# Pair sums of w_up made during attention and kept in HBM, and five pairs by seven products in four up chunks

## The chip, the cores and the metric

The kernel runs on one core of one Trainium2 chip. A time is the device time of one execution in microseconds (us). The five engines of the core (TensorE or PE, VectorE or DVE, ScalarE or ACT, GpSimd or POOL, SyncE or SP) each take their own list of instructions in order; semaphores join them. TensorE writes to PSUM, 8 banks of 512 float32 in each of 128 partitions; the other data lie in SBUF.

## The reference

One decoder layer over 256 tokens of width 2048, all in float32:

```python
h = _rmsnorm(x, norm_attn_pre)
proj = h @ w_in                      # 2048 x 4160: A.q, A.k, A.v, c_q, c_kv, k_rope
...                                  # A: dilated window attention, B: latent attention, 8 heads each
x = x + _rmsnorm(mixed @ w_out, norm_attn_post)
h = _rmsnorm(x, norm_mlp_pre)
u = jnp.square(jax.nn.relu(h @ w_up))          # w_up 2048 x 8192
x = x + _rmsnorm(u @ w_down, norm_mlp_post)    # w_down 8192 x 2048
```

## The kernel before, in words

**Products in three passes.** Each float32 matrix is split into a rounded part `hi` and a rest `lo`: ScalarE makes `hi` (L293, with a gain L297), VectorE makes `lo` (L294, with a gain L298). A product is three matmuls, hi by hi, hi by lo and lo by hi (`three`, L983).

**The weight stream.** `Weights` (L154) holds a list of all weight tiles of the program in order of use, each 128 x 1024. `emit` (L178) loads a tile on SP's queue into one of five `raw` buffers and writes its split into one of eight pairs of `hi` and `lo`; `get` (L209) does that for the tile in use and the six after it. So the loads and splits of a tile stand in the lists of their engines where TensorE is six tiles earlier.

**Stages.** First come the projection of x, the heads of A beside the later projections, the latent projections with the heads of B beside them, and the product with w_out. Then follow the up stage and the down stage. The up stage computes h @ w_up in eight chunks of 1024 columns (`j`), each over 16 tiles of 128 rows (`k`); the results of a chunk lie in four banks (two token blocks, two halves of 512 columns).

**Seven products.** In chunks 1 to 7 rows 2k and 2k+1 of w_up for k = 0, 1, 2 are taken as a pair: a 2 x 2 product of blocks (two row tiles by two token blocks by two halves) is made of seven block products instead of eight (`seven_products`, L988), each by three passes. That needs sums of blocks on both sides. The left sums, of h, are made once, in chunk 0, by `left_sums` (L958); they also put the gain into h for the rows they cover (L965). The right sums, of the weights, are made for each pair in each chunk by `seven` (L333): two row tiles are loaded on POOL's queue into the tile `ab` (L360), VectorE makes `t` (L345) and then `u` (L349, L350), and four tiles of the weight stream are made from them: half of the first row tile, the second row tile, u and t. Four extra banks `m` collect those products that several blocks share, and `close` (L1002) adds them up behind the last pair of a chunk; `up_evac` (L905) then adds the result to the accumulators, takes relu, has TensorE transpose it and squares it. `UP_STEPS` (L97) is the order in chunks 1 to 7: plain tiles 6 to 10, pair 0, 11, 12, pair 1, 13, pair 2, 14, 15. A plain tile is 12 matmuls, a pair 21.

**What sets the order.** The schedule is written by hand. `Flow` (L115) runs chains of small steps (Python generators) beside the main line of matmuls; a step yields the number of us, in a rough clock that adds a constant for each matmul, after which its next step is put into the program. All engine lists follow from that clock, which only places instructions and does not time them on the chip. `prelude` (L531) loads x into the tiles `xs`; `powers` (L811) scales them by powers of two before `residual` (L832) adds the attention's result.

Of the kernel before, what the change touches and what calls it, by code (L numbers as in the profile page):

```python
# [18 lines left out]
F32 = mybir.dt.float32  # L19
F32R = mybir.dt.float32r  # L20
# [74 lines left out]

N_SEVEN, SUMS_AHEAD = 3, 2
UP_STEPS = [("k", k) for k in range(6, 11)]  # L97
for _i, _n in enumerate(((11, 12), (13,), (14, 15))):
    UP_STEPS += [("w", _i)] + [("k", k) for k in _n]

# [150 lines left out]
def layer(nc, tc, io):  # L251
# [78 lines left out]

    late = {}

    def seven(load, targets):  # L333

        st, tt, H = {}, nc.vector.tensor_tensor, 512

        def sums():
            ab = load()  # L340
            a, b = st["a"], st["b"] = [ab[:, :CW], ab[:, CW:]] if not isinstance(ab, list) else ab
            t, u = st["t"], st["u"] = targets()
            if not isinstance(ab, list):
                two = [x.rearrange("p (k n) -> p k n", n=H) for x in (t, ab)]
                tt(out=two[0], in0=two[1][:, 0:2, :], in1=two[1][:, 1:4:2, :], op=OP.add)  # L345
            else:
                for x, o in ((a, 0), (b, H)):
                    tt(out=t[:, o:o + H], in0=a[:, o:o + H], in1=x[:, H:], op=OP.add)
            tt(out=u[:, :H], in0=t[:, :H], in1=b[:, H:], op=OP.add)  # L349
            tt(out=u[:, H:], in0=u[:, :H], in1=b[:, :H], op=OP.add)  # L350
# [12 lines left out]
    def seven_up(j, kp):  # L363
        def load():
            if j == FF // CW - 1 and kp:
                return [weights.load(up_weight(j, 2 * kp + i), CW, f"raw_w{j}_{kp}{i}") for i in range(2)]
            return load_two(late["ab"], nc.gpsimd if (j, kp) > (1, 0) else nc.sync,
                            io["w_up"][2 * kp * P:(2 * kp + 2) * P, j * CW:(j + 1) * CW])

        return seven(load, lambda: [late["up"].tile([P, CW], F32, tag="T", bufs=2, name=f"{n}{j}_{kp}") for n in "tu"])  # L370
# [30 lines left out]
    wide_u, after = [], 0  # L401
    for j in range(FF // CW):
        wide_u.append([])
        for what, k in [("k", k) for k in range(KD)] if j == 0 else UP_STEPS:
            if what == "k":
                ts = [weights.plan(up_weight(j, k), 1, CW, gcol[:, 8 + k:9 + k])]
# [124 lines left out]
    def prelude():  # L531
# [15 lines left out]
        rstd0.append(rstd_of(ss0, NB, D, "pre"))  # L547

    def tables():

# [98 lines left out]

    pre = flow.start(prelude())  # L650
    tab = flow.start(tables())
    heads, evacs = [], []
    for half in range(2):
# [157 lines left out]
    def powers():  # L811
# [93 lines left out]
    def up_evac(j, b, i, acc, order, more=None):  # L905
# [11 lines left out]
        if j not in uT:  # L917
            if j in (12, 13):
                t2 = late["ab"][:, (j - 12) * CW:(j - 11) * CW]
            else:  # L920
# [37 lines left out]
    def left_sums(kp):  # L958
# [7 lines left out]
        four_sums(q, f)  # L966
        st = [late["st"][:, i * 512:(i + 1) * 512] for i in (2 * kp, 2 * kp + 1)]
        yield 3.0
# [19 lines left out]
    def seven_products(ts, left, accs, m, first, last):  # L988
# [4 lines left out]
        for p, (a, i, half, to) in enumerate(prods):  # L993
            w = weights.get(ts[i])
# [21 lines left out]
    for j in range(FF // CW):  # L1016
# [9 lines left out]
        for t, b in order:  # L1026
            what, k, tiles = steps[t]
            if (j, t, b) == (0, 8, 0):
# [11 lines left out]
            if j == 1 and what == "w":  # L1040
                flow.until(lambda: len(sums) > k)
# [12 lines left out]

            first, last = k == 0, k == N_SEVEN - 1
            if first:
# [205 lines left out]
```

## Time and profile before

| | us |
|---|---|
| median of 3 runs | 1055.2 (1055.2 to 1055.52) |
| span of the profiled execution | 1053.8 |
| TensorE busy | 1040.8 |
| VectorE busy | 811.1 |
| ScalarE busy | 625.1 |
| GpSimd busy | 61.5 |

The span runs from the first to the last instruction that was profiled. Matmuls overlap in the pipeline, so a single one reads some 0.39 us where the next starts after 0.23. In the lists of groups a line ends with busy time, mean ns of one, and the idle time of the engine ahead of it with what ended it. In a table of windows the columns are the window, its length, then for each engine the busy time with the number of instructions, the granted clock of TensorE, the share of the DMA engines that was busy, and GB/s.

### The profile page before, as it was taken

What the parts mean: (1) busy time and instruction counts of PE and PEld (TensorE: products, weight loads), DVE (VectorE), ACT (ScalarE), POOL (GpSimd) and SP (SyncE); (2) the same over time, 40 slices, a digit from 0 to 9 for tenths busy, and PEclk for the clock granted to TensorE, in tenths of its full rate; (3) what the DMA queues carried; (4) which work ended last, traced back from release to release, by engine and by line L of the source; (5) the groups of instructions that cost most, each with busy time, mean ns of one, the idle gap of its engine ahead of it and who ended that gap; (6) DMA issues with size and microseconds to landing.
All of it is one profiled execution on the core that took longest, in us unless ns stands there. A gap on an engine that the chain in (4) does not pass through costs nothing.

```text
span 1053.8 us, 13458 instructions
## 1 busy us (share of the span) xinstructions
PE 1040.8 (99%) x4854; PEld 867.4 (82%) x4854; DVE 811.1 (77%) x1080; ACT 625.1 (59%) x834; POOL 61.5 (6%) x116
## 2 busy tenths in 40 slices
PE   9999999999999999999999999999999999999996
PEld 6888889888888788888888888888888888888884
DVE  6676536567557679879888798887899987989994
ACT  6584536565555467566665666566666664666671
POOL 0000000000000000000000100000000001212100
PEclk9999999999999999999999999999999999999998
DMA  9974447454447295647556466469779767789952
GB/s 296 361 233 146 143 130 241 143 162 159 140 171 231 78 347 167 224 142 239 185 198 200 154 222 217 139 223 318 256 274 317 263 216 271 254 297 327 375 167 80
DMA packets 80644, 229.34 MB, mean 218 GB/s; under 512 B 7617, under 2 KB 12225, under 8 KB 80193
## 3 DMA queue, kind: packets, MB, share of 16 engines
q1 hardware_dynamic: 65888, 176.45, 49.3%
q0 software_dynamic: 14112, 51.39, 14.2%
q8 instruction: 38, 0.62, 0.2%
q10 hardware_dynamic: 576, 0.64, 0.2%
q14 instruction: 30, 0.24, 0.1%
HBM read 212.72 MB, written 15.73 MB: 217 GB/s over the span
## 4 chain that ended last, share of the span: by engine, by line
PE 96%; DVE 1%; issue 1%; DMA 0%; ACT 0%; POOL 0%; DVEq 0%; POOLq 0%; ACTq 0%
PE y L283 26%; PE acc_u L283 25%; PE acc_o L283 8%; PE m L283 5%; PE md L283 5%; PE acc_qk L283 4%; PE acc_v L283 4%; PE acc_ckv L283 2%; PE acc_ukv L283 2%; PE acc_q L283 2%; PE acc_cq L283 2%; PE acc_k L283 2%; PE acc_uq L283 2%; PE rt L287 1%; PE sc_b L283 1%
## 5 line engine op out<-in xcount | busy, mean ns | idle before, releaser
L294 DVE TENSOR_TENSOR lo<-raw,hi 128x1024 fp32r<-128x1024 f32 (+3 forms) x213 | 241.8, 1152 | 92.5 <-ACT hi L293 91.9
L293 ACT ACTIVATE hi<-raw 128x1024 fp32r<-128x1024 f32 (+3 forms) x213 | 209.4, 999 | 78.3 <-PE y L283 20.8
L283 PE MATMUL acc_u<-hi,hT_hi 128*128 128x512 f32 x386 | 153.4, 397 | 0.0
L283 PE MATMUL acc_u<-hi,hT_lo 128*128 128x512 f32 x386 | 150.9, 391 | 0.4 <-DVE hT_lo L294 0.4
L283 PE MATMUL acc_u<-lo,hT_hi 128*128 128x512 f32 x386 | 150.5, 390 | 0.0
L283 PE MATMUL y<-hi,uhi 128*128 128x512 f32 x376 | 146.6, 390 | 0.0
L283 PE MATMUL y<-hi,ulo 128*128 128x512 f32 x376 | 146.3, 389 | 0.0
L283 PE MATMUL y<-lo,uhi 128*128 128x512 f32 x376 | 146.3, 389 | 0.0
L298 DVE SCALAR_TENSOR_TENSOR lo<-raw,gcol,hi 128x1024 fp32r<-128x1024 f32 x86 | 107.6, 1281 | 10.6 <-ACT hi L297 10.3
L297 ACT ACTIVATE hi<-raw,gcol 128x1024 fp32r<-128x1024 f32 x86 | 97.6, 1151 | 26.6 <-PE acc_u L283 13.2
L283 PEld LDWEIGHTS acc_u<-hi,hT_lo 128*128 128x128 f32 x386 | 72.5, 188 | 16.1 <-DVE hT_lo L294 0.8
L283 PEld LDWEIGHTS acc_u<-hi,hT_hi 128*128 128x128 f32 x386 | 72.6, 188 | 14.3 <-DVE c L1008 0.4
L283 PEld LDWEIGHTS acc_u<-lo,hT_hi 128*128 128x128 f32 x386 | 72.6, 188 | 14.2
L283 PEld LDWEIGHTS y<-hi,ulo 128*128 128x128 f32 x376 | 70.6, 188 | 14.6
L283 PEld LDWEIGHTS y<-hi,uhi 128*128 128x128 f32 x376 | 70.6, 188 | 14.6
L283 PEld LDWEIGHTS y<-lo,uhi 128*128 128x128 f32 x376 | 70.6, 188 | 14.5
L283 PE MATMUL acc_o<-hi,mixT_hi 128*128 128x512 f32 x128 | 51.8, 405 | 0.0
L294 DVE TENSOR_TENSOR lo<-st_down,hi 128x1024 fp32r<-128x1024 f32 x40 | 48.1, 1221 | 4.0 <-ACT hi L293 3.8
L283 PE MATMUL acc_o<-hi,mixT_lo 128*128 128x512 f32 x128 | 50.2, 392 | 0.0
L283 PE MATMUL acc_o<-lo,mixT_hi 128*128 128x512 f32 x128 | 50.0, 391 | 0.0
L293 ACT ACTIVATE hi<-st_down 128x1024 fp32r<-128x1024 f32 x40 | 42.1, 1052 | 11.1 <-PE y L283 9.5
L293 ACT ACTIVATE hi<-ab 128x512 fp32r<-128x512 f32 (+1 forms) x38 | 31.9, 842 | 28.2 <-PE acc_u L283 21.7
(322 smaller groups left out, 1989.3 us busy)
## 6 DMA issues: line engine op xcount, KB each, us to landing
raw<-in_w_down SPq DMA_DIRECT2D x88, 512.0 KB, 6.2
raw<-in_w_up SPq DMA_DIRECT2D x86, 512.0 KB, 4.5
raw<-in_w_in SPq DMA_DIRECT2D x55, 512.0 KB, 5.0
ab<-in_w_up POOLq DMA_DIRECT2D x36, 512.0 KB, 4.8
raw<-in_w_out SPq DMA_DIRECT2D x32, 512.0 KB, 4.4
ab_down<-in_w_down POOLq DMA_DIRECT2D x20, 512.0 KB, 6.7
ukeep<-ulo SPq DMA_DIRECT2D x15, 512.0 KB, 7.2
ulo<-ukeep POOLq DMA_DIRECT2D x15, 512.0 KB, 5.3
```

The costliest lines, as they stand in the source:

```text
L283: nc.tensor.matmul(out, a, b, start=start, stop=stop)
L287: nc.tensor.transpose(out, a, ident)
L293: nc.scalar.activation(hi, src, AF.Copy)
L294: nc.vector.tensor_tensor(out=lo, in0=src, in1=hi.bitcast(F32), op=OP.subtract)
L297: nc.scalar.activation(hi, src, AF.Copy, scale=g)
L298: nc.vector.scalar_tensor_tensor(out=lo, in0=src, scalar=g, in1=hi.bitcast(F32), op0=OP.mult, op1=OP.subtract)
```

## The change

The pairs of chunks 1 to 5 are named in an order for each chunk, with a new kind of step `p`: a pair whose right sums were made earlier. Chunk 1 has three such pairs (0, 1, 2), chunks 2 to 5 have four (0 to 3) and one pair (4) that is summed on the spot as before; chunks 6 and 7 keep their three pairs summed on the spot. That makes 3 + 4 x 4 = 19 prepared pairs. Left sums are now made for five pairs, so rows 6 to 9 of h carry the gain from chunk 2 on, and plain tiles of those rows are split without it.

```diff
+UP_STEPS = {0: [("k", k) for k in range(KD)]}
+UP_STEPS[1] = steps_of("k6 k7 k8 k9 k10 p0 k11 k12 p1 k13 p2 k14 k15")
+for _j in range(2, 6):
+    UP_STEPS[_j] = steps_of("k10 k11 k12 p0 k13 p1 w4 k14 p2 p3 k15")
+for _j in range(6, NUP):
+    UP_STEPS[_j] = steps_of("k6 k7 k8 k9 k10 w0 k11 k12 w1 k13 w2 k14 k15")
+SCALED = {1: range(6), **{j: range(10) for j in range(2, NUP)}}
+PREP = [(j, k) for j in UP_STEPS for w, k in UP_STEPS[j] if w == "p"]
+D_PREP = (8.0, 1.3, 0.8, 0.8)
...
+    def pair_sums(ab, t, u):
+
+        H, tt = 512, nc.vector.tensor_tensor
+        two = [x.rearrange("p (k n) -> p k n", n=H) for x in (t, ab)]
+        tt(out=two[0], in0=two[1][:, 0:2, :], in1=two[1][:, 1:4:2, :], op=OP.add)
+        yield D_PREP[1]
+        tt(out=u[:, :H], in0=t[:, :H], in1=ab[:, 3 * H:], op=OP.add)
+        yield D_PREP[2]
+        tt(out=u[:, H:], in0=u[:, :H], in1=ab[:, 2 * H:3 * H], op=OP.add)
+        yield D_PREP[3]
...
+            elif what == "p":
+                kept = sums_kept[j, k]
+                ts = [weights.plan(src, 1, n) for src, n in (
+                    (up_weight(j, 2 * k)[:, :512], 512), (up_weight(j, 2 * k + 1), CW),
+                    (kept[:, CW:], CW), (kept[:, :CW], CW))]
...
+    def prepare():
+
+        ab, tu = xs
+        while pre in flow.chains:
+            yield 0.5
+        for j, kp in PREP:
+            load_two(ab, nc.gpsimd, io["w_up"][2 * kp * P:(2 * kp + 2) * P, j * CW:(j + 1) * CW])
+            yield D_PREP[0]
+            yield from pair_sums(ab, tu[:, :CW], tu[:, CW:])
+            nc.gpsimd.dma_start(out=sums_kept[j, kp], in_=tu)
+        yield 2.0
+        for b in range(NB):
+            nc.gpsimd.dma_start(out=xs[b], in_=io["x"][b * P:(b + 1) * P, :])
...
+    prep = flow.start(prepare())
...
+        while prep in flow.chains:
+            yield 0.5
+        yield 8.0
         for b in range(NB):
             for c in (slice(0, CW), slice(CW, D)):
                 nc.vector.tensor_scalar_mul(xs[b][:, c], xs[b][:, c], pw[:, b:b + 1])
...
-    def all_sums():
-        for kp in range(N_SEVEN - 1):
+    def some_sums(kps, after=0.0):
+        yield after
+        for kp in kps:
             yield from left_sums(kp)
-        yield 8.0
-        yield from left_sums(N_SEVEN - 1)
...
-                flow.start(all_sums())
+                late["st2"] = late["up"].tile([P, 2 * CW], F32R, tag="uT10", bufs=1, name="st2")
+                flow.start(some_sums((0, 1)))
+                flow.start(some_sums((2,), 18.0))
+            if (j, t, b) == (1, 4, 0):
+                flow.start(some_sums((3, 4), 6.0))
```

The sums use the two tiles of x (`xs`) between the sum of squares of x and the residual: the first as `ab`, the second for t and u. x is loaded again afterwards. The left sums of pairs 3 and 4 lie in the place of `uT10` and `uT11`.

How the lists of the engines change is shown at three places. First VectorE beside the heads of A, at the heads 1 and 3 of the first half. `qkT_a` is the transposed q and k that the score matmul waits for, `lo` the split of a weight tile, `mixT_lo` the rest of an earlier head's result. Before:

```order
L628 COPY qkT_a_894<-qkT_a_889 128x512
L294 TENSOR_TENSOR lo_899<-raw_896,hi_898 128x1024
L294 TENSOR_TENSOR mixT_lo<-o_a_908,mixT_hi 128x256
L628 COPY qkT_a_918<-qkT_a_913 128x512
L593 ISA s_a_926,st_a_927<-sc_a_923,cst 128x128
```

and now, with x_136 as `ab` and x_137 as the tile of t and u:

```order
L673 COPY qkT_a_927<-qkT_a_922 128x512
L352 TENSOR_TENSOR x_137<-x_136 128x1024
L308 TENSOR_TENSOR lo_933<-raw_930,hi_932 128x1024
L308 TENSOR_TENSOR mixT_lo<-o_a_942,mixT_hi 128x256
L354 TENSOR_TENSOR x_137<-x_137,x_136 128x512
L673 COPY qkT_a_953<-qkT_a_948 128x512
L356 TENSOR_TENSOR x_137<-x_137,x_136 128x512
L638 ISA s_a_962,st_a_963<-sc_a_958,cst 128x128
```

Two of the three sum operations of a pair now stand between the two copies, and the first of them waits for the transfers of that pair.

Second, POOL from the latents to the norm behind attention. Before:

```order
L485 TENSOR_TENSOR rstd_q<-t_q,neg_half 128x2
L710 MEMSET krT 128x512
L485 TENSOR_TENSOR rstd_pw<-t_pw,neg_half 128x2
L485 TENSOR_TENSOR rstd_post_3196<-t_post_3195,neg_half 128x1
L485 TENSOR_TENSOR rstd_post_3312<-t_post_3311,neg_half 128x1
```

and now, at the last two pairs (the store of the sums, the next pair's loads, the reloads of x):

```order
L589 DMA sums_2_87<-x_137 128x2048
L386 DMA x_136<-in_w_up 128x1024 x2
L589 DMA sums_3_88<-x_137 128x2048
L592 DMA x_136<-in_x 128x2048
L592 DMA x_137<-in_x 128x2048
L516 TENSOR_TENSOR rstd_pw<-t_pw,neg_half 128x2
```

A store, the loads behind it and the reload of x now stand ahead of `rstd_pw` on POOL's list.

Third, VectorE at the end of chunk 2 of the up stage, where `c` is the closing of the seven products and `acc_u` its addition to the accumulators. Before:

```order
L345 TENSOR_TENSOR t_0_4348<-ab 128x1024
L349 TENSOR_TENSOR u_0_4349<-t_0_4348,ab 128x512
L350 TENSOR_TENSOR u_0_4349<-u_0_4349,ab 128x512
L298 SCALAR_TENSOR_TENSOR lo_4356<-raw_4353,gcol,hi_4355 128x1024
L1008 TENSOR_TENSOR c<-m_2_4175,c 128x512
L1008 TENSOR_TENSOR c<-m_2_4176,c 128x512
L1008 TENSOR_TENSOR c<-m_2_4177,c 128x512
L1008 TENSOR_TENSOR c<-c,m_2_4176 128x512
L298 SCALAR_TENSOR_TENSOR lo_4373<-raw_4370,gcol,hi_4372 128x1024
L294 TENSOR_TENSOR lo_4389<-ab,hi_4388 128x512
L294 TENSOR_TENSOR lo_4409<-ab,hi_4408 128x1024
L909 TENSOR_TENSOR acc_u_00_4041<-acc_u_00_4041,c 128x512
```

and now:

```order
L312 SCALAR_TENSOR_TENSOR lo_4522<-raw_4519,gcol,hi_4521 128x1024
L308 TENSOR_TENSOR lo_4534<-raw_4531,hi_4533 128x512
L308 TENSOR_TENSOR lo_4546<-raw_4543,hi_4545 128x1024
L1061 TENSOR_TENSOR c<-m_2_4278,c 128x512
L1061 TENSOR_TENSOR c<-m_2_4279,c 128x512
L1061 TENSOR_TENSOR c<-m_2_4280,c 128x512
L1061 TENSOR_TENSOR c<-c,m_2_4279 128x512
L308 TENSOR_TENSOR lo_4563<-raw_4560,hi_4562 128x1024
L308 TENSOR_TENSOR lo_4585<-raw_4582,hi_4584 128x1024
L958 TENSOR_TENSOR acc_u_00_4195<-acc_u_00_4195,c 128x512
```

The sums ahead of the closing are gone from this place, and two splits instead of three stand between it and the first addition.

More of the change, by code (lines that the diff above doesn't have):

```diff
@@ L93, with steps_of @@
 D_UP, UP_STEP = 1.8, 2.2
[L96 to L99, printed above, removed]
+SUMS_AHEAD = 2
+NUP = FF // CW
+def steps_of(text):
+    return [(s[0], int(s[1:])) for s in text.split()]
+UP_STEPS = {0: [("k", k) for k in range(KD)]}
[7 more added lines that the diff above has]
+D_PREP = (8.0, 1.3, 0.8, 0.8)
 DOWN_SEVEN = ((7, 11, 13, 17, 19, 23, 25, 29), (4, 7, *range(9, 28, 2)))
@@ L331, in layer @@
     late = {}
+    sums_kept = {jk: dram.tile([P, 2 * CW], F32, name=f"sums{jk[0]}_{jk[1]}") for jk in PREP}
+    def pair_sums(ab, t, u):
[7 more added lines that the diff above has]
+        yield D_PREP[3]
     def seven(load, targets):
@@ L343, in sums @@
             if not isinstance(ab, list):
[L344 to L348, printed above, removed]
+                for _ in pair_sums(ab, t, u):
+                    pass
+                return
+            for x, o in ((a, 0), (b, H)):
+                tt(out=t[:, o:o + H], in0=a[:, o:o + H], in1=x[:, H:], op=OP.add)
             tt(out=u[:, :H], in0=t[:, :H], in1=b[:, H:], op=OP.add)
@@ L366, in load @@
                 return [weights.load(up_weight(j, 2 * kp + i), CW, f"raw_w{j}_{kp}{i}") for i in range(2)]
-            return load_two(late["ab"], nc.gpsimd if (j, kp) > (1, 0) else nc.sync,
-                            io["w_up"][2 * kp * P:(2 * kp + 2) * P, j * CW:(j + 1) * CW])
+            return load_two(late["ab"], nc.gpsimd, io["w_up"][2 * kp * P:(2 * kp + 2) * P, j * CW:(j + 1) * CW])
         return seven(load, lambda: [late["up"].tile([P, CW], F32, tag="T", bufs=2, name=f"{n}{j}_{kp}") for n in "tu"])
@@ L401, in layer @@
     wide_u, after = [], 0
-    for j in range(FF // CW):
+    for j in range(NUP):
         wide_u.append([])
-        for what, k in [("k", k) for k in range(KD)] if j == 0 else UP_STEPS:
+        for what, k in UP_STEPS[j]:
             if what == "k":
-                ts = [weights.plan(up_weight(j, k), 1, CW, gcol[:, 8 + k:9 + k])]
+                g = () if k in SCALED.get(j, ()) else (gcol[:, 8 + k:9 + k],)
+                ts = [weights.plan(up_weight(j, k), 1, CW, *g)]
+            elif what == "p":
[3 more added lines that the diff above has]
+                    (kept[:, CW:], CW), (kept[:, :CW], CW))]
             else:
@@ L919, in up_evac @@
                 t2 = late["ab"][:, (j - 12) * CW:(j - 11) * CW]
+            elif j in (10, 11):
+                if j == 10:
+                    late["uT10"] = late["up"].tile([P, 2 * CW], F32, tag="uT10", bufs=1, name="uT10")
+                t2 = late["uT10"][:, (j - 10) * CW:(j - 9) * CW]
             else:
@@ L966, in left_sums @@
         four_sums(q, f)
-        st = [late["st"][:, i * 512:(i + 1) * 512] for i in (2 * kp, 2 * kp + 1)]
+        sp, i0 = (late["st"], 2 * kp) if kp < 3 else (late["st2"], 2 * kp - 6)
+        st = [sp[:, i * 512:(i + 1) * 512] for i in (i0, i0 + 1)]
         yield 3.0
@@ L993, in seven_products @@
         for p, (a, i, half, to) in enumerate(prods):
-            w = weights.get(ts[i])
+            w = [x[:, 0, :] if len(x.shape) == 3 else x for x in weights.get(ts[i])]
             in_m = isinstance(to, int)
@@ L1039, in layer @@
                 u_next = split_u(0, 0)
-            if j == 1 and what == "w":
+            if what != "k":
                 flow.until(lambda: len(sums) > k)
@@ L1053, in layer @@
                 continue
-            first, last = k == 0, k == N_SEVEN - 1
+            pairs = [s[1] for s in steps if s[0] != "k"]
+            first, last = k == pairs[0], k == pairs[-1]
             if first:
```

## The prediction

> **What bounds the kernel now.** First the page's head, its chain of waits and the list of what TensorE waited for.
>
> ```profile
> span 1053.8 us, 13458 instructions
> PE 1040.8 (99%) x4854; PEld 867.4 (82%) x4854; DVE 811.1 (77%) x1080; ACT 625.1 (59%) x834; POOL 61.5 (6%) x116
> PE 96%; DVE 1%; issue 1%; DMA 0%; ACT 0%; POOL 0%; DVEq 0%; POOLq 0%; ACTq 0%
> PE warm L505 <- DVE zero L502: 1.2, 1, 1.2
> PE acc_qk L283 <- ACT hi L293: 0.7, 1, 0.7
> PE acc_u L283 <- DVE hT_lo L294: 0.4, 1, 0.4
> PE qrt L287 <- DVE qT L744: 0.2, 1, 0.2
> ```
>
> TensorE is the bound: 96% of the chain, and 2.5 us of waiting in all. So a matmul less is its time less, and anything that makes TensorE wait is added whole. The chain in order of time prices a matmul:
>
> ```profile
> 571.17 10.88 PE acc_u L283 x48
> 596.89 5.44 PE acc_u L283 x24
> ```
>
> 10.88/48 = 0.2267 us each, when they follow one another.
>
> **Part 1, the matmuls.** A pair of row blocks takes 24 matmuls as two plain tiles (2 tiles, 2 token blocks, 2 halves, 3 passes) and 21 as seven products. Chunks 2 to 5 go from three such pairs to five, so 4 x 2 x 3 = 24 matmuls go (4574 rows on TensorE become 4550): 24 x 0.2267 = **-5.4 us**. Nothing in TensorE's list is added.
>
> **Part 2, nineteen pair sums on VectorE during attention.** Each is three operations:
>
> ```profile
> L345 DVE TENSOR_TENSOR t<-ab 128x1024 f32<-128x1024 f32 x19 | 23.2, 1222 | 17.2 <-DMA ab<-in_w_up 17.2
> L349 DVE TENSOR_TENSOR u<-t,ab 128x512 f32<-128x512 f32 x19 | 13.2, 692 | 0.7
> L350 DVE TENSOR_TENSOR u<-u,ab 128x512 f32<-128x512 f32 x19 | 13.2, 693 | 0.6
> 62.00:320.00 258.00, 257.81 (x1346) 222.24 (x1345) 155.08 (x311) 142.57 (x261) 2.57 (x4) 1.00 0.51 166
> 69.87 3.49 DVE L294 TENSOR_TENSOR lo<-raw,hi 128x1024 fp32r<-128x1024 f32 x3
> 315.87 1.23 DVE L294 TENSOR_TENSOR lo<-raw,hi 128x1024 fp32r<-128x1024 f32 x1 [0.25 <-ACT hi L293]
> ```
>
> 1.222 + 0.692 + 0.693 = 2.6 us, 19 times: 49.5 us. By the place of the weight splits around them in VectorE's list, the first sum falls between the second and third split of the 69.87 row (72.1) and the last just ahead of the one at 315.87: 18 spacings of (315.9 - 72.1)/18 = 13.5 us. In that window VectorE was busy 155 of 258 us; 204.6 of 258 is 79%. So the work itself fits in idle time; without that cover it would be 49.5 us.
>
> What matters is what stands behind a sum. VectorE takes its list in order, and the sum waits for three transfers: the 1 MB store of the last sums (its target is the same tile) and the two 512 KB loads. All three are issued only when the last sum is done, so each pair is one serial loop: landing time L, then the sum. L is not in this trace; the nearest rows:
>
> ```profile
> GB/s 389 397 393 397 397 393 393 397 377 393 373 377 389 393 389 385 381 381 389 377 311 352 389 299 274 340 328 221 184 160 311 315 111 45 0 53 78 311 401 316
> raw<-in_w_out SPq DMA_DIRECT2D x14, 512.0 KB, 3.6
> ab<-in_w_up POOLq DMA_DIRECT2D x36, 512.0 KB, 4.8
> 604.20 0.54 POOL L360 DMA_DIRECT2D ab<-in_w_up  x1 [8.87 <-DVE lo L294]
> 605.33 0.54 POOL L360 DMA_DIRECT2D ab<-in_w_up  x1 [0.60 <-DVE lo L294]
> ```
>
> The engines move 393 GB/s when full (40 to 60 us). 512 KB landed alone in 3.6 us (200 to 265 us): 1.3 of bytes, 2.3 fixed. The 2.10 MB of a pair alone: 2.3 + 5.3 = 7.6, the lower bound. With SP's weight loads taking every second turn: 2.3 + 10.7 = 13.0, the upper. The nearest row is a pair in the up stage: two loads 1.13 us apart, 4.8 to land, 1.05 MB in 5.9 us beside plain weight loads; less 2.3 that is 290 GB/s, and 2.10 MB then take 9.5. I take L = 9.5. Free for it are 13.5 less the sum (2.6) and the one split between its parts (1.2): 9.7. So it just fits on average. The spacing is uneven, though: the second sum stands right behind this split,
>
> ```profile
> 80.61 1.22 DVE L294 TENSOR_TENSOR lo<-raw,hi 128x1024 fp32r<-128x1024 f32 x1
> 98.81 0.68 DVE L628 COPY qkT_a<-qkT_a 128x512 f32<-128x512 f32 x1
> 101.04 0.38 PE L283 MATMUL sc_a<-qkT_a 128*128 128x128 f32 x2
> ```
>
> at 81.8, 9.7 us after the first, so VectorE will stand some 3.6 us there. Weights are split six tiles ahead (12 matmuls, 2.7 us each: 16 us) and do not feel that. The attention heads do: a score matmul came 1.55 us after its copy (99.49 to 101.04), and ahead of that copy now stand 1.22 + 0.69 us of a sum, less what idle time takes up. I charge 0.3 us at each of four such places: **+1.2 us**. Bounds: 0, if the other idle time absorbs it, and the loop of the first rival.
>
> Bytes: 19 x 2.10 MB over 245 us is 163 GB/s on top of 166, 329 of 393: 84%.
>
> **Part 3, the up stage.** VectorE in one chunk, and the splits:
>
> ```profile
> 527.77:571.17 43.40, 43.40 (x201) 35.92 (x200) 37.08 (x40) 27.51 (x32) 3.23 (x6) 1.00 0.59 196
> L298 DVE SCALAR_TENSOR_TENSOR lo<-raw,gcol,hi 128x1024 fp32r<-128x1024 f32 x86 | 107.6, 1281 | 10.6 <-ACT hi L297 10.3
> L294 DVE TENSOR_TENSOR lo<-ab,hi x38: 683/955/1227, 404.7 to 665.3; 128x512 fp32r<-128x512 f32 x19, 128x1024 fp32r<-128x1024 f32 x19
> L293 ACT ACTIVATE hi<-raw 128x1024 fp32r<-128x1024 f32 (+3 forms) x213 | 209.4, 999 | 78.3 <-PE y L283 20.8
> raw<-in_w_down SPq DMA_DIRECT2D x88, 512.0 KB, 6.2
> ```
>
> Chunks 2 to 5 lose two sums (5.2) and four plain splits (5.1) and gain two pairs of splits (2 x (0.68 + 3 x 1.22) = 8.7): 37.1 - 1.6 = 35.5 of 42.0 us, no tighter. The right sums now come through SP's queue and the five raw buffers: a prepared pair loads 1.84 MB for 21 matmuls, a chunk 11.5 MB in 42 us, 274 GB/s instead of 196. If loads land in 6.2 us, as in the down stage, a raw buffer turns round in 6.2 + 1.0 + 1.2 = 8.4 us, 1.68 per tile with five, against 4.76/4 = 1.19 that TensorE takes. Over the eight tiles of pairs 2 and 3 that is 3.9 us behind, out of a lead of six tiles (7.1 us): hidden.
>
> Closing a chunk moves: the seven products end one plain tile (2.72 us) before the chunk's end, not two.
>
> ```profile
> 573.82 2.28 DVE L1008 TENSOR_TENSOR c<-m,c 128x512 f32<-128x512 f32 x3
> 576.13 0.69 DVE L1008 TENSOR_TENSOR c<-c,m 128x512 f32<-128x512 f32 x1
> 579.67 0.69 DVE L909 TENSOR_TENSOR acc_u<-acc_u,c 128x512 f32<-128x512 f32 x1
> 580.40 0.69 ACT L912 ACTIVATE r<-acc_u,rstd_pre 128x512 f32<-128x512 f32 x1 [2.63 <-DVE acc_u L909]
> 581.90 0.27 PE L287 MATMUL rt<-ident,r 128*128 128x128 f32 x1
> ```
>
> The last product ended at 571.17 and closing began 2.65 us later, since 2.6 us of sums stood ahead of it; the transpose came 0.8 us after its input. Now no sums stand there: closing starts some 0.7 late (my estimate, between 0 and 2.65), takes 3.0, then two splits (2.4) and the add: 3.4 us after the chunk's end, where it was 3.1 (579.67, less the end at 571.17 + 5.44). Inside the 0.8 of slack in most chunks: **+0.4 us** for four, between 0 and 4 x 1.2.
>
> **Part 4, x again.** x is reloaded once the sums are done, and the power of the norm waits on POOL behind that:
>
> ```profile
> 320.83 1.60 POOL L485 TENSOR_TENSOR rstd_pw<-t_pw,neg_half 128x2 f32<-128x2 f32 x1 [112.69 <-DVE t_pw L484]
> 350.36 2.08 DVE L841 SCALAR_TENSOR_TENSOR x<-yg,rstd_post,x 128x512 f32<-128x512 f32 x3 [0.66 <-POOL rstd_post L485]
> ```
>
> The second reload waits for the last store, so this power comes some 7 us late and holds VectorE about 4 us near 325. TensorE has 16 us of split weights there and needs x only at 350: nothing. Without that cover it is the 4 us.
>
> **The sum.** 1053.8 - 5.4 + 1.2 + 0.4 = 1050.0 of span. The span is 1.4 under the median of the runs, 1055.2: forecast **1051.4 us**. About 2 us (0.2%) can be told from no change, so faster is below 1053.1, slower above 1057.3.
>
> **Rivals.** (a) All hidden: 1055.2 - 5.4 = 1049.8. For it: the 40% of idle VectorE time; against: the 1.55 us of slack. (b) Sums cost more at the score steps: at 0.3 us for each of 16 heads, 4.8 us, nothing is left: 1054.6, no change. (c) The serial loop decides. At L = 13.0 a pair needs 16.8 us against 13.5, 3.3 more for each; it decides from L above 9.7. Over the seven pairs between 62 and 100 and between 150 and 200, where weight loads are densest, this is 23 us less about 5 of slack at their starts: 1055.2 - 5.4 + 18 = 1068. Against it stands the up stage's pair at 290 GB/s. The Trainium skill (DMA: Bandwidth & Descriptors, Queues, rings and completion order) says that an engine takes turns between the queues it has work for, which is that half share; in the trace POOL's pair got more than half, because SP's queue was often empty. (d) The raw buffers fall behind: 3.9 us at each of four chunks if the lead is already spent, 15.6 - 5.4: 1065. (e) POOL's issues wait for VectorE: three issues per pair, each held by one 1.22 us operation, make L 9.5 + 3.7 = 13.2, and all 18 loops 3.5 too long: 63 us, 1113. In the trace an issue took 0.54 us with VectorE 85% busy, so hardly. The Trainium skill (SBUF — State Buffer, two separate sides) has the rule: VectorE's two-port modes lock GpSimd out of writing descriptors; no row here shows it.
>
> **Chances.** Forecast 0.38, (a) 0.25, (b) 0.13, (c) 0.17, (d) 0.06, (e) 0.01. Faster 0.63, same 0.13, slower 0.24. The forecast's own range, with give-backs from 0.6 to 3.3, is 1050.4 to 1053.1; ranged over (a), (b) and the milder part of (c), 1049.4 to 1061.
>
> **What will show it.** 24 matmuls fewer, chunks 2 to 5 at about 42.0 us each. In the waits, VectorE behind the pair transfers for 5 to 25 us in all, and TensorE behind VectorE in attention for about 1 us more; over 40 us and over 5 us would be (c). TensorE waiting for `hi` or `lo` in chunks 2 to 5 would be (d), for `rt` the closing. Wrong altogether if attention ends more than 4 us later.

## The result, and the profile after

| | before | changed |
|---|---|---|
| median of the runs, us | 1055.2 | 1092.9 (1088.5 to 1095.3) |
| ratio | | 1.0358, 95% interval 1.0343 to 1.0373 |
| profiled execution: span, us | 1053.8 | 1089.3 |
| first `acc_q` matmul to first `acc_u` matmul (attention and w_out) | 282.8 | 318.0 |
| first `acc_u` matmul to first `y` matmul (up stage) | 351.3 | 355.4 |

The kernel became 3.6% slower where 0.4% faster was forecast. The two rows of stages, from the starts of the tiles' first matmuls, say where: 35.2 us in attention, 4.1 in the up stage, which was to gain 5.4. What lies ahead of `acc_q` and behind the first `y` took 1.7 and 2.1 less: the first `acc_q` matmul started between 70.9 and 72.9 us in all profiled executions of this document, and the 2.1 us lie at the program's end, behind the last operation of VectorE (see e8).

First the page's head and its chain, as shown for the kernel before:

```profile
span 1089.3 us, 13736 instructions
PE 1051.1 (96%) x4830; PEld 869.8 (80%) x4830; DVE 847.5 (78%) x1136; ACT 637.6 (59%) x854; POOL 80.3 (7%) x155
PE 62%; DMA 15%; issue 9%; DVE 9%; ACT 2%; POOL 1%; DVEq 0%; POOLq 0%; ACTq 0%
```

The 24 matmuls are gone (4830 rows instead of 4854). But TensorE is 62% of the chain where it was 96%, and transfers are 15% where they were 0: TensorE now waits. For whom, say the waits of TensorE, and of VectorE (the line that waits, whom for, us in total, times, the longest):

```profile
PE pT_a L301 <- DVE s_a L649: 8.6, 3, 4.1
PE acc_u L297 <- DVE c L1061: 5.0, 5, 1.5
PE qrt L301 <- DVE qr L630: 4.2, 2, 3.9
PE pT_b L301 <- DVE s_b L649: 3.7, 1, 3.7
PE acc_o L297 <- DVE mixT_lo L308: 2.2, 1, 2.2
PE sc_a L297 <- DVE qkT_a L673: 1.9, 1, 1.9
DVE x L352 <- DMA x<-in_w_up: 46.1, 16, 7.4
```

The attention's steps wait, nearly all for VectorE (21.9 us with the small ones, 0.2 before), and VectorE stood 46.1 us behind the loads of the pairs, at 16 of 19 sums. The second row is the closing of a chunk in the up stage. One place in attention where a pair is late, in the chain in order of time (start, length, what):

```profile
183.32 9.99 DMA x<-in_w_up
193.39 1.23 DVE x L352
...
195.37 0.59 DVE x L354
...
197.45 0.60 DVE x L356
...
199.93 1.22 DVE lo L308
...
201.27 0.30 DVE s_a L649
201.56 0.14 issue
201.70 0.87 PE pT_a L301 x3
```

The second load of a pair lands 10.0 us after its issue. VectorE takes its list in order and comes to the sum at 190.27; it stands 3.12 us until the load is there, then makes the sum. A softmax row `s_a` stands behind it, and a transpose on TensorE behind that. What TensorE does around the wait, in the timeline:

```profile
196.96 0.39 PE L297 MATMUL acc_cq<-lo,xT_hi 128*128 128x512 f32 x1
197.19 0.39 PE L297 MATMUL acc_cq<-hi,xT_lo 128*128 128x512 f32 x1
201.70 0.87 PE L301 MATMUL pT_a<-ident,s_a 128*128 128x128 f32 x3 [4.12 <-DVE s_a L649]
...
203.22 0.63 PE L297 MATMUL acc_cq<-hi,xT_lo 128*128 128x512 f32 x1
203.65 0.63 PE L297 MATMUL acc_cq<-hi,xT_hi 128*128 128x512 f32 x1
```

It starts a matmul every 0.23 us ahead of the wait and every 0.43 behind it. So this wait costs twice: itself, and some microseconds at half the clock. The windows show it as granted clock (the column ahead of the DMA share); before, it was 1.00, and here too from 150 to 200 us:

```profile
62.00:100.00 38.00, 34.02 (x155) 27.98 (x154) 24.84 (x46) 18.95 (x30) 5.11 (x9) 0.96 0.81 277
100.00:150.00 50.00, 48.06 (x215) 39.53 (x214) 33.21 (x57) 21.55 (x35) 4.72 (x9) 0.97 0.76 268
200.00:265.00 65.00, 58.77 (x276) 49.80 (x277) 44.80 (x83) 34.32 (x66) 7.63 (x14) 0.90 0.81 273
265.00:320.00 55.00, 50.46 (x257) 43.14 (x256) 36.79 (x82) 25.19 (x49) 4.72 (x9) 0.97 0.76 262
320.00:360.00 40.00, 37.81 (x164) 30.63 (x164) 26.39 (x41) 20.01 (x36) 4.20 (x8) 0.96 0.81 292
```

In the trace's record of the clock this is eight slots of 3.41 us at half rate, 27.3 us in all. For 3.7 us of them TensorE stood in waits that are already counted; half of the other 23.6 is 11.8 us lost. With the 21.9 of waits that is 33.7 of the attention's 35.2. The Trainium skill (TensorE: Matmul & The Clock Gate, Part 1: The HAM clock gate) has it that after an idle window of about 3.4 us the array gets half its clock until it has been busy for as long. This wait agrees, with 4.12 us of idle time and half rate until 206.47, 4.8 us behind its end. The two waits in the last section do not follow that length, and there the measurement decides.

The rate of the pairs, from the view of the tile `x` (durations, first and last start):

```profile
L352 DVE TENSOR_TENSOR x<-x x19: 1217/1226/1227, 71.1 to 349.8; 128x1024 f32<-128x1024 f32 x19
```

(349.8 - 71.1)/18 = 15.5 us from sum to sum, where 13.5 was planned. Over the 17 pairs between the first store issue (75.06) and the eighteenth (336.55), from store issue to the landing of the second load it took 10.2 us on average (8.5 to 12.3), and from there to the next store issue 5.2.

### The profile page after: what moved, and what is told of

The parts are those of the page before. It is cut to its first block, busy times and chain, and to the rows that moved or that the text cites. A ratio compares the mean times of both kernels' runs of the same rounds, so it can differ in the third digit from the quotient of the medians.

```text
span 1089.3 us, 13736 instructions
## 1 busy us (share of the span) xinstructions
PE 1051.1 (96%) x4830; PEld 869.8 (80%) x4830; DVE 847.5 (78%) x1136; ACT 637.6 (59%) x854; POOL 80.3 (7%) x155
## 4 chain that ended last, share of the span: by engine, by line
PE 62%; DMA 15%; issue 9%; DVE 9%; ACT 2%; POOL 1%; DVEq 0%; POOLq 0%; ACTq 0%
PE y L297 25%; PE acc_u L297 18%; DMA x<-in_w_up 10%; PE md L297 5%; PE acc_o L297 5%; PE m L297 4%; DMA raw<-in_w_up 4%; DVE lo L308 2%; PE acc_cq L297 1%; PE rt L301 1%; ACT hi L307 1%; DVE lo L312 1%; DVE x L352 1%; DVE c L1061 1%; PE acc_k L297 1%
## 5 line engine op out<-in xcount | busy, mean ns | idle before, releaser
L308 DVE TENSOR_TENSOR lo<-raw,hi 128x1024 fp32r<-128x1024 f32 (+3 forms) x297 | 331.9, 1137 | 89.0 <-ACT hi L307 87.9
L307 ACT ACTIVATE hi<-raw 128x1024 fp32r<-128x1024 f32 (+3 forms) x297 | 289.6, 988 | 122.6 <-DMA raw<-in_w_in 25.0
L297 PE MATMUL acc_u<-hi,hT_hi 128*128 128x512 f32 x338 | 135.4, 401 | 5.4 <-DVE c L1061 5.0
L297 PE MATMUL acc_u<-hi,hT_lo 128*128 128x512 f32 x338 | 132.6, 392 | 0.4 <-DVE hT_lo L308 0.4
L297 PE MATMUL acc_u<-lo,hT_hi 128*128 128x512 f32 x338 | 132.4, 392 | 0.0
L312 DVE SCALAR_TENSOR_TENSOR lo<-raw,gcol,hi 128x1024 fp32r<-128x1024 f32 x62 | 78.6, 1281 | 11.1 <-ACT hi L311 10.7
L297 PEld LDWEIGHTS y<-hi,uhi 128*128 128x128 f32 x376 | 70.6, 188 | 14.5
L311 ACT ACTIVATE hi<-raw,gcol 128x1024 fp32r<-128x1024 f32 x62 | 70.7, 1150 | 17.8 <-DMA raw<-in_w_up 14.0
L297 PEld LDWEIGHTS acc_u<-hi,hT_lo 128*128 128x128 f32 x338 | 63.8, 189 | 14.5 <-DVE hT_lo L308 0.9
L297 PE MATMUL m<-hi,st 128*128 128x512 f32 x174 | 64.5, 394 | 0.0
L352 DVE TENSOR_TENSOR x<-x 128x1024 f32<-128x1024 f32 x19 | 23.3, 1225 | 46.1 <-DMA x<-in_w_up 46.1
```

Source lines behind the costliest of these rows:

```text
L297: nc.tensor.matmul(out, a, b, start=start, stop=stop)
L307: nc.scalar.activation(hi, src, AF.Copy)
L308: nc.vector.tensor_tensor(out=lo, in0=src, in1=hi.bitcast(F32), op=OP.subtract)
L311: nc.scalar.activation(hi, src, AF.Copy, scale=g)
L312: nc.vector.scalar_tensor_tensor(out=lo, in0=src, scalar=g, in1=hi.bitcast(F32), op0=OP.mult, op1=OP.subtract)
```

## The experiments

Theory 1, for attention: store, two loads and sum are one loop on one pair of buffers. It takes longer than its room, VectorE stands in it, and each pair pushes all that is behind it. Rivals: the 49.5 us of added VectorE work; the added traffic. Theory 2, for the up stage: the closing `c` has too little room. Rival: the raw loads are late. All runs (stages in us as in the first table; ratios to the kernel before on the same chip):

| run | attention | up | time | ratio (95%) |
|---|---|---|---|---|
| before | 282.8 | 351.3 | 1055.2 | |
| changed | 318.0 | 355.4 | 1092.9 | 1.0343 to 1.0373 |
| e1 sums alone | 286.5 | 356.9 | 1063.4 | 1.0063 to 1.0093 |
| e2 transfers alone | 282.8 | 358.1 | 1060.0 | 1.0032 to 1.0062 |
| e3 up alone | 282.8 | 355.8 | 1059.3 | 1.0028 to 1.0062 |
| e4 two buffers | 286.4 | 358.5 | 1063.6 | 1.0067 to 1.0097 |
| e5 e4, two plain tiles | 286.5 | 350.8 | 1057.9 | 1.0018 to 1.0037 |
| e6 e3, seven raw | 283.7 | 351.0 | 1054.4 | 0.9984 to 1.0003 |
| e7 one buffer, more room | 283.8 | 357.6 | 1059.6 | 1.0026 to 1.0055 |
| e8 e5, seven raw | 287.0 | 347.2 | 1052.5 | 0.9963 to 0.9984 |
| e9 e8, sixteen pairs | 285.7 | 349.7 | 1053.7 | 0.9980 to 0.9998 |
| e10 changed, up of e8 | 310.6 | 346.2 | 1077.4 | 1.0198 to 1.0226 |
| e11 before, seven raw | 283.7 | 353.4 | 1058.1 | 1.0019 to 1.0044 |
| e12 e8, fifteen pairs | 286.6 | 347.7 | 1053.0 | 0.9968 to 0.9986 |
| e13 e8 again | 287.0 | 346.8 | 1053.4 | 0.9975 to 0.9992 |

e1, e2, e3, e6 and e7 do without the sums or the loads of some pairs, and so compute something else than the layer.

**e1: sums without transfers.**

```diff
-                kept = sums_kept[j, k]
+                kept = sums_kept[PREP[0]]
...
-            load_two(ab, nc.gpsimd, io["w_up"][...])
+            if (j, kp) == PREP[0]:
+                load_two(ab, nc.gpsimd, io["w_up"][...])
...
-            nc.gpsimd.dma_start(out=sums_kept[j, kp], in_=tu)
+            if (j, kp) == PREP[0]:
+                nc.gpsimd.dma_start(out=sums_kept[j, kp], in_=tu)
```

> All nineteen pair sums are made in their places in VectorE's list, but only the first pair is loaded and stored; the other eighteen sum the same data again and nothing waits for a transfer (the prepared pairs of the up stage all read the first pair's sums, so the output is another one). Theory (the loop of store, two loads and sum on one buffer runs slower than its 13.5 us of room, and VectorE stands in it with the score steps behind it): the attention and out stages get their time back, the first up matmul starts at 355 to 358 us instead of 388.9, VectorE waits under 5 us for the pair transfers, the granted clock is 0.99 to 1.00 between 200 and 265 us, and the time is 1058 to 1062 us, since the up stage keeps its loss of about 4. Rival 1 (49.5 us more of VectorE work is by itself too much for the score steps): the first up matmul still after 375 us, the time over 1080. Rival 2 (the traffic slows the weight loads): the same as the theory here.

The attention is 3.7 us longer than before, not 35.2, and the granted clock was 1.00 in all its windows there. So the VectorE work is not what the change costs, though it is not free: 3.0 us of waits in five places (`mixT_lo` 0.9, `qr` 0.7, `qT` 0.6, `s_a` 0.5, `kb` 0.3). The time came out 1.4 above the upper end expected, and the first `acc_u` matmul 0.6.

**e2: transfers without sums.**

```diff
-            yield from pair_sums(ab, tu[:, :CW], tu[:, CW:])
+            if (j, kp) == PREP[0]:
+                yield from pair_sums(ab, tu[:, :CW], tu[:, CW:])
+            else:
+                yield D_PREP[1] + D_PREP[2]
+                nc.vector.memset(tu[:, :1], 0.0)
+                yield D_PREP[3]
```

> All loads and stores of the nineteen pairs are issued, but eighteen of the sums are left out: a one-column fill stands for each sum, at the end of its place, and paces the store (the kept sums are not right). Theory: VectorE still stands until the store of the pair before has landed (the fill writes the stored tile), but not for the two loads and not for the 2.6 us of sums, so the loop store, loads is no longer closed through VectorE: most of the loss is gone, first up matmul at 356 to 364 us, time 1058 to 1068. Rival 1 (VectorE's work): as the theory. Rival 2 (40 MB of loads and 20 MB of stores slow the weight loads in SP's queue and TensorE waits for splits): first up matmul still after 375 us, the time over 1078, and TensorE waiting behind DMA or hi and lo.

The window of 200 to 265 us in this run:

```profile
200.00:265.00 65.00, 64.81 (x351) 56.91 (x350) 43.37 (x103) 39.20 (x77) 9.14 (x17) 1.00 0.93 329
```

329 GB/s with the DMA engines 93% busy, and TensorE as full as in e3, which moves 154 GB/s there. The attention takes 282.8 us, as before. (The traffic is 20 MB of loads and 20 MB of stores, not the 40 and 20 named there.) So the traffic alone costs nothing and the work alone 3.7 us; the loss is in their being tied together.

**e3: the up stage alone.**

```diff
-        for j, kp in PREP:
+        for j, kp in PREP[:1]:
...
-                kept = sums_kept[j, k]
+                kept = sums_kept[PREP[0]]
```

> Only the first of the nineteen pairs is prepared, and all the prepared pairs of the up stage read its kept sums (the output is another one). So attention is nearly that of before and the up stage is wholly that of the change. Theory (two separate losses: 33.5 us in attention and out stage, and some 4 us in the up stage where 5.4 were to be gained): first up matmul at 355 to 357 us, and the time 1055.2 + 4 = 1057 to 1061 us. Rival (the up stage's loss comes out of the late attention: loads that are behind, a clock that was lowered): the up stage gains its 5.4 us, 1049 to 1051 us.

The attention is that of before, and the up stage loses all the same, 4.5 us. So the up stage's loss is its own, 9.9 us above what 24 matmuls fewer would give (-5.4), and not an echo of the late attention.

**e4: two buffers.** The sums are made in place (the second row tile is loaded with its halves swapped, so that each operation writes what it has just read), and the two tiles take turns.

```diff
-        ab, tu = xs
...
+        load(0)
+        load(1)
+        yield D_PREP[0]
...
+        for i, jk in enumerate(PREP):
+            x = xs[i % 2]
+            two = x.rearrange("p (k n) -> p k n", n=H)
+            tt(out=two[:, 0:2, :], in0=two[:, 0:2, :], in1=two[:, 1:3, :], op=OP.add)
+            yield D_PREP[1]
+            tt(out=x[:, 2 * H:3 * H], in0=x[:, :H], in1=x[:, 2 * H:3 * H], op=OP.add)
+            yield D_PREP[2]
+            tt(out=x[:, 3 * H:], in0=x[:, 2 * H:3 * H], in1=x[:, 3 * H:], op=OP.add)
+            yield D_PREP[3]
+            nc.gpsimd.dma_start(out=sums_kept[jk], in_=x)
+            yield D_PREP[0]
+            if i + 2 < len(PREP):
+                load(i + 2)
```

> The same nineteen sums and the same bytes, but the three operations write into the loaded tile itself, and the two 1 MB tiles take turns: the loads of pair i+2 are issued right behind the store of pair i, and the sums of pair i+1 do not wait for that. A pair's transfers then have about 27 us less the sum, instead of 13.5. Theory (the closed loop on one buffer): nearly all of the attention's loss is gone, VectorE waits under 8 us for the pair loads, first up matmul at 356 to 361 us, granted clock 0.98 or more between 200 and 265 us, time 1058 to 1064 us. Rivals (VectorE's work alone; traffic): no better than half way, first up matmul after 372 us, time over 1075.

The wait of VectorE for pair loads:

```profile
DVE x L598 <- DMA x<-in_w_up: 0.3, 1, 0.3
```

and the window of 200 to 265 us:

```profile
200.00:265.00 65.00, 63.29 (x343) 55.19 (x341) 51.94 (x109) 38.41 (x75) 11.42 (x21) 1.00 0.86 298
```

46.1 us of waiting became 0.3, the clock 1.00, and the attention 286.4 us: what e1 took without any transfer. All sums and all bytes are there; opening the loop was worth 31.6 of the 35.2 us.

**e7: the same loop with more room.** One pair of buffers as in the change, thirteen pairs instead of nineteen (the other six prepared pairs read the first one's sums).

```diff
-D_PREP = (8.0, 1.3, 0.8, 0.8)
+D_PREP = (13.0, 1.3, 0.8, 0.8)
+N_PREP = 13
...
-        for j, kp in PREP:
+        for j, kp in PREP[:N_PREP]:
```

> The changed kernel with its single pair of buffers, but the room between two sums is about 18 to 20 us instead of 13.5 and thirteen pairs are prepared instead of nineteen (the other six prepared pairs of the up stage read the first pair's sums). The loop took 14.5 us in the changed kernel. Theory (a loop that is longer than its room adds its excess at every pair): with more room than loop nothing adds up, VectorE waits under 15 us for the pair transfers instead of 46, the first up matmul comes at 356 to 361 us instead of 388.9, up stage 355 to 359, time 1058 to 1064. Rival (each wait of VectorE at a pair costs, however wide the room): 13/19 of the 33.5 us, first up matmul at about 378 and the time at about 1082.

(The loop of the changed kernel took 15.4 to 15.5 us, not the 14.5 named there.) The view of the tile `x`:

```profile
L353 DVE TENSOR_TENSOR x<-x x13: 1217/1218/1221, 75.3 to 295.4; 128x1024 f32<-128x1024 f32 x13
```

and the window of 200 to 265 us:

```profile
200.00:265.00 65.00, 64.67 (x349) 56.61 (x348) 50.68 (x108) 39.47 (x77) 6.02 (x11) 1.00 0.78 267
```

(295.4 - 75.3)/12 = 18.3 us of room for each pair, no wait of VectorE for a pair in the list, and 1.0 us of loss in place of 35.2; 13/19 of that would have been 24. The clock was 1.00 here too. With 18.3 us of room the loop costs next to nothing; it is the excess over the room that adds up.

**e5 and e6: the two readings of the up stage.** e5 is e4 with one line changed, e6 is e3 with one line changed:

```diff
-    UP_STEPS[_j] = steps_of("k10 k11 k12 p0 k13 p1 w4 k14 p2 p3 k15")
+    UP_STEPS[_j] = steps_of("k10 k11 k12 p0 k13 p1 w4 p2 p3 k14 k15")
```

```diff
-RAW_BUFS, W_BUFS, W_AHEAD, AHEAD_NORM = 5, 8, 6, 4
+RAW_BUFS, W_BUFS, W_AHEAD, AHEAD_NORM = 7, 7, 6, 4
```

> e4_two_buffers with one line of the up stage changed: in chunks 2 to 5 the last two prepared pairs stand ahead of both plain tiles 14 and 15, so 5.44 us of plain tiles lie between the last product and the chunk's end, not 2.72. The result is the reference's. In e4 the up stage took 358.5 us (first up matmul to first down matmul), in the kernel before 351.3, and by 24 matmuls fewer it would be 345.9; the loss sits at the ends of chunks 2 to 5, where the next chunk's first matmuls wait for the closing (6.6 us in six waits) and the granted clock falls to 0.96 in the last. Theory (the closing c stands in VectorE's list behind the splits of the next tiles, and one plain tile is too little room for it): waits behind c under 2 us, up stage 347 to 351 us, time 1052 to 1056. Rival (the raw loads fall behind by themselves; the order of tiles only moves the wait): TensorE waits behind hi and lo of p2 and p3 instead, up stage over 354, time over 1059.

> e3_up_alone with seven raw buffers instead of five and seven pairs of split buffers instead of eight, so that loads are issued up to two tiles earlier; the order of tiles is that of the change. Only the first pair is prepared and all prepared pairs read its kept sums. In e3 the up stage took 355.8 us. Rival of the order theory (loads late, so splits late, so closing late): up stage 346 to 351 us, waits behind c under 2 us, time 1050 to 1055. Order theory: the same 355 to 357 us, since c still stands behind the same splits and one plain tile.

Each edit shortened the up stage as its own theory said, and each theory was wrong in holding that the other edit would change little: the order took 7.7 us off the up stage (358.5 to 350.8), the buffers 4.8 (355.8 to 351.0). The time of e5 still came out 1.9 above its range; its profiled execution was the shortest of ten (1055.8). The end of chunk 5 in the changed kernel shows why they are one thing. The chain in order of time, then VectorE's timeline:

```profile
635.85 7.23 DMA raw<-in_w_up
...
645.69 4.97 DMA raw<-in_w_up
...
652.95 1.28 DVE lo L312
654.23 0.61 DVE c L1061
...
657.20 4.97 PE acc_u L297 x14
```

```profile
645.57 3.74 DVE L308 TENSOR_TENSOR lo<-raw,hi 128x1024 fp32r<-128x1024 f32 x3
649.23 1.22 DVE L352 TENSOR_TENSOR t<-ab 128x1024 f32<-128x1024 f32 x1
...
651.82 1.22 DVE L308 TENSOR_TENSOR lo<-raw,hi 128x1024 fp32r<-128x1024 f32 x1
652.95 1.28 DVE L312 SCALAR_TENSOR_TENSOR lo<-raw,gcol,hi 128x1024 fp32r<-128x1024 f32 x1
654.15 2.28 DVE L1061 TENSOR_TENSOR c<-m,c 128x512 f32<-128x512 f32 x3
656.46 0.69 DVE L1061 TENSOR_TENSOR c<-c,m 128x512 f32<-128x512 f32 x1
```

The last product started at 648.94, yet the operations of `c` on VectorE begin at 654.15. Ahead of it in VectorE's list stand the splits of tiles up to six ahead and the sums of chunk 6's first pair, and the splits wait for raw loads of 5 to 7 us. The next chunk writes its accumulators into the banks that `c` reads, so its first matmuls wait too, twice 1.3 to 1.5 us here, and the clock falls (one slot of 3.41 us at half rate, 0.96 from 615 to 663 us). Earlier loads move `c` forward; a second plain tile moves the need for it back.

**e8: both.**

> e5_two_plain with seven raw buffers and seven pairs of split buffers as well; the result is the reference's. If room behind the last product and early loads both count, this is the faster of the two: up stage 346 to 348 us, first up matmul at 357 to 359, time 1051 to 1054, below the kernel before. If the order alone does it, the same as e5 within 1 us; if seven split buffers are too few, TensorE waits for hi and lo and the time is above e5's.

Chunks 2 to 5 in the windows of this run:

```profile
454.80:497.10 42.30, 42.30 (x194) 34.72 (x193) 36.04 (x39) 29.91 (x35) 1.05 (x2) 1.00 0.82 283
497.10:539.40 42.30, 42.30 (x194) 34.74 (x193) 35.84 (x38) 29.90 (x35) 1.05 (x2) 1.00 0.78 272
539.40:581.70 42.30, 42.30 (x194) 34.74 (x193) 35.88 (x38) 30.04 (x35) 1.05 (x2) 1.00 0.80 278
581.70:625.30 43.60, 42.70 (x195) 34.57 (x193) 37.75 (x40) 29.87 (x35) 2.12 (x4) 1.00 0.77 263
```

42.3 us for three of four, where the prediction had 42.0: nearly the gain that was asked for. With 1052.5 us this is 0.26% below the kernel before, and e13, the same kernel once more, gave 0.17%. But the stages do not show where that comes from: the up stage takes 4.1 us less than before, and the attention 4.2 us more. VectorE's last operation before and in e8:

```profile
1046.31 1.54 DVE L1104 SCALAR_TENSOR_TENSOR uT<-uT,rstd_fin,uT 128x512 f32<-128x512 f32 x3
1046.47 1.54 DVE L1180 SCALAR_TENSOR_TENSOR uT<-uT,rstd_fin,uT 128x512 f32<-128x512 f32 x3
```

It ends 0.16 us later in e8 (in e13 0.65 earlier), yet the span is 1051.8 us instead of 1053.8. What is shorter is the program's end, the closing semaphores behind the last store: GpSimd's came 2.04 us behind SyncE's last one in the kernel before, and 0.03 in e8. From the start of the last matmul to the end of the span it is 10.9 us in both traces of the kernel before's code (before, e11) and 8.5 to 9.7 in all others; why was not tried. So in these traces the prepared pairs, with the better order and the buffers, come out even with the kernel before, within 0.7 us.

**e11: the control.** The line of e6 in the kernel before.

> The kernel before, with seven raw buffers and seven pairs of split buffers and nothing else. Control for e8: there TensorE waited only 2.5 us in all, so earlier loads have nothing to give: 1054.5 to 1056, no difference that can be told. If it is faster by 2 us or more, then e8's gain is the buffers' and not the prepared sums'.

It is slower by 0.31%, outside the range expected: a chunk takes 43.9 us instead of 43.4. It has one pair of split buffers fewer; whether that is the cause was not tried. So the buffers alone are not what shortens e8's up stage.

**e10: the loop left in.** The changed kernel with both lines of e5 and e6.

> The changed kernel with the loop on one pair of buffers left as it is, and the up stage of e8_order_raw7 (two plain tiles behind the last pair, seven raw and seven pairs of split buffers). If the two losses are separate: first up matmul at 386 to 391 us as in the changed kernel (388.9), up stage 346 to 349 us as in e8 (347.0), time 1081 to 1087. If the late attention feeds the up stage's loss, or seven raw buffers shorten the waits in attention, first up matmul before 384 or up stage over 351.

The up stage is that of e8 (346.2), as expected, so the up stage's loss does not come from the late attention. The attention is 7.4 us shorter than in the changed kernel, which the expectation put down to the rival, that the raw buffers shorten the waits there; the time, 1077.4, lies under the range. VectorE stood 32.9 us behind pair loads instead of 46.1 and TensorE waited 19.3 us instead of 21.9; the larger part, some 5 us, is the clock, five slots at half rate instead of eight. Whether the buffers or the shifted places in the lists did that was not separated.

**e9 and e12: fewer sums.** e9 forms chunk 1's pairs in place, e12 those of chunk 5; the room is wider accordingly.

```diff
-UP_STEPS[1] = steps_of("k6 k7 k8 k9 k10 p0 k11 k12 p1 k13 p2 k14 k15")
+UP_STEPS[1] = steps_of("k6 k7 k8 k9 k10 w0 k11 k12 w1 k13 w2 k14 k15")
-D_PREP = (8.0, 1.3, 0.8, 0.8)
+D_PREP = (10.0, 1.3, 0.8, 0.8)
```

```diff
-for _j in range(2, 6):
+for _j in range(2, 5):
...
-for _j in range(6, NUP):
+for _j in range(5, NUP):
...
-D_PREP = (8.0, 1.3, 0.8, 0.8)
+D_PREP = (10.8, 1.3, 0.8, 0.8)
```

> e8_order_raw7 with chunk 1 as in the kernel before (its three pairs formed in place; prepared pairs save no matmul there), so sixteen pairs are prepared instead of nineteen, with about 16 us between two sums instead of 13.5; the result is the reference's. In e8 the first up matmul came at 359.6 us (355.4 in the kernel before), in e7 with thirteen pairs 18.3 us apart at 356.1. If the sums' work costs by how many stand ahead of score steps: first up matmul at 357 to 358.5, up stage 347 to 349, time 1049.5 to 1052. If chunk 1 has not enough VectorE time for five left sums and three pairs in place: chunk 1 longer than 47.1 us and the time above 1053.

> e8_order_raw7 with chunk 5 as chunks 6 and 7 (three pairs formed in place), so fifteen pairs are prepared, about 17 us apart, and chunk 1 keeps its prepared pairs (e9 showed 49.5 us for it without them, against 46.7). Five pairs stand in chunks 2 to 4 alone: 18 matmuls fewer than before, not 24. If the attention's share falls with the number of sums: first up matmul at 357 to 358.5 (359.6 in e8), up stage 347.5 to 349 (347.0 in e8, where chunk 5 ended with a wait of 1.3 us), time 1050.5 to 1052.5, at or below e8. If not: first up matmul still at 359 or later and the time 1053 to 1055.

> e8_order_raw7 once more, unchanged, beside e12 on the same chip: 1052.5, between 1050 and 1054.5, first up matmul 358.5 to 360.

Neither beats e8 by anything that can be told. In e9 chunk 1 took 49.5 us, so its prepared pairs earn their place though they save no matmul. In e12 fifteen sums cost as much in attention (286.6) as nineteen (287.0), while e7's thirteen on one buffer cost 1.0. So the number of sums does not set this rest of some 3 us; which place in the list does is open.

## Why the prediction was wrong, step by step

**Part 1** held: 24 matmuls went (the page has 4854 and 4830 rows, not the 4574 and 4550 named), and where nothing else stood in the way (e8) a chunk took 42.3 us against 42.0.

**Part 2** is the step that failed: "So it just fits on average." Two sizes were a little short, and their sum is what decided. The landing time L was taken as 9.5 us; it was 10.2. Between landing and the next store, 2.6 of sums and one split of 1.2 were counted; it was 5.2, since more of VectorE's list lies between the three operations (softmax steps and splits of `mixT_lo` of 0.48 us in the place shown). 15.4 instead of 13.3, against a room of 13.5. Then the form of the charge: 0.3 us at four places treats a late pair as one wait that ends there. In a closed loop every pair is late by the excess: 18 x (15.5 - 13.5) = 36 us, near the 35.2 that were lost. With the room at 18.3 (e7) or the loop opened (e4) it is gone. The prediction's own sign of being wrong altogether, attention more than 4 us late, came: the first `acc_u` matmul started 33.5 us later.

The work of the sums without the loop, forecast at +1.2, was 3.6 to 3.7 (e1, e4), more than the 3.3 that the forecast's own range left for all give-backs. The places were also others: the score matmul behind `qkT_a`, whose slack of 1.55 us was weighed, is not among the waits of e1.

**Rival (c)** named the mechanism, the point from which it decides (L above 9.7), and the rows that would show it, TensorE over 5 us behind VectorE and VectorE over 40 behind pair transfers: 21.9 and 46.1. Its price of 18 us was half of what came: it took 3.3 us for each late pair, where 2.0 came, but held only seven of nineteen pairs to be late. And 0.17 was little for a limit of 9.7 against an L of 9.5.

**What no part had** is the clock. All prices of waits were their own length; 11.8 of 33.7 us in attention were matmuls at half rate around them.

**Part 3** failed in its slack. The raw buffers "3.9 us behind, out of a lead of six tiles: hidden" holds for TensorE's own tiles, which never waited for `hi` or `lo`. But `c` stands in VectorE's list behind the splits of that lead, so what the loads lose, the closing loses. And the closing was held against the transpose `rt`, 3.4 us after the chunk's end, where the first to need it is the next chunk's matmul into the banks that `c` reads. "Now no sums stand there" was wrong for chunk 5, behind which chunk 6 forms its first pair. The +0.4 was 9.9 in e3; e5 and e6 show that room and loads both count.

**Part 4** was right in what counts: VectorE stood 6.1 us behind the power (4 forecast), and TensorE waited for nothing there.

**Rivals (d) and (e).** (d), raw buffers behind, is about half of the up stage's loss (4.8 of 9.9 in e6), though not through `hi` and `lo`. (e) did not come: POOL's issues took 0.53 us each (median of 38).

## What to carry to other kernels

A transfer and an operation that wait for each other on one buffer form a loop; compare its whole turn (all landings, and everything in the engine's list between landing and the next issue) with its room, and if it does not clear that with margin, the excess counts once for every turn. Here a second buffer opened it (e4, 31.6 us). For work that stands behind look-ahead splits in an in-order list, such as a closing, the lead of the splits is no slack: find the first reader of the banks it frees, and leave room for what stands ahead of it.

## What the runs showed of the hardware

Half rate goes not by the length of a wait alone. In the changed kernel it followed a wait of 1.94 us (score matmul `sc_a` behind `qkT_a`, until 107.18); in e10 the same step waited 3.02 us (until 105.26) and full rate went on. The record of the granted clock says more. From the first `acc_q` matmul to the last matmul of a trace half rate comes only in stretches of 3.41 or 6.83 us, and in the changed kernel the seven stretches, which start at 93.83, 107.48, 199.64, 257.67, 305.45, 336.17 and 657.03 us, lie whole multiples of 3.413 us apart. So there the clock was set for slots of 3.413 us, on a grid that does not move with the waits. The slots around the two waits (window, length, TensorE's busy time with its matmuls, granted clock, DMA share, GB/s), first in the changed kernel, then in e10:

```profile
100.66:104.07 3.41, 3.41 (x21) 1.00 0.97 370
104.07:107.48 3.41, 1.47 (x8) 1.00 0.22 34
107.48:110.89 3.41, 3.41 (x10) 0.50 0.96 355
```

```profile
100.73:104.14 3.41, 1.51 (x7) 1.00 0.51 189
104.14:107.55 3.41, 2.29 (x11) 1.00 0.65 204
107.55:110.97 3.42, 3.42 (x17) 1.00 0.99 293
```

The shorter wait lies within one slot, and the next is at half rate. The longer one lies across two, and none is. Over all fifteen traces, the slot ahead of a stretch of half rate had TensorE busy for 5 to 53% of its time, and no slot with 59% or more led to one. In between, slots with 44 and 52% in e10 did not, and with 46, 47 and 53% in e1, e4 and e6 did, so this busy time, whose ends are modelled, is not the whole measure; what is stays open. A slot at half rate was followed by another where TensorE was busy for 79% of it or less, and by full rate from 95% on. The end of chunk 5 has two such slots in e1, e2, e4 and e7 and one in the changed kernel, e3 and e6, which is 1.7 us of the difference among their up stages.
